# Seven products in three more places, and one step more ahead of the first scores, in a two-layer hybrid encoder

## The chip, the core and the metric

The kernel runs on one core of one Trainium2 chip. The metric is the device time of one execution in microseconds. Three runs of the kernel before took 2244.38, 2242.65 and 2243.16 us, so the median is 2243.16.

## What is computed

A trunk of two layers over 256 positions of width 2048, all in fp32: RMS-normalisation, a token mixer and a residual add, then RMS-normalisation, a gated MLP with a convolution of width 3 over positions and a residual add. Layer 0 mixes by grouped-query attention (mixer A: 16 query heads, 4 key and value heads of 128, RMS-normalised and rotated queries and keys), layer 1 by three groups of 8 heads with dilated windows (mixer B). At the end stands one more RMS-normalisation. Cut to the skeleton:

```python
def reference(x, ...):
    h = x
    for i in range(2):
        hn = rms_norm(h, mix_norm[i])
        h = h + (mixer_a(hn, ...) if i == 0 else mixer_b(hn, ...))
        h = h + conv_ffn(rms_norm(h, ffn_norm[i]), ...)
    return rms_norm(h, final_norm)

def mixer_b(h, w_qkv, w_o, rel_bias):
    qkv = (h @ w_qkv).reshape(b, s, 3, 3, 8, 128)       # group, q/k/v, head
    ...
    return y @ w_o

def conv_ffn(h, w_up, conv_w, conv_b, w_down):           # 2048 -> 2 x 5632 -> 2048
    u = conv(h @ w_up) + conv_b
    gate, val = jnp.split(u, 2, axis=-1)
    return (silu(gate) * val) @ w_down
```

## The kernel before

**Matmuls.** An fp32 matmul is made of three in the fp32r type: both operands are split in a high and a low part, and hi·hi, hi·lo and lo·hi are summed in a PSUM bank. Weights come in tiles `raw` of 128x1024 by DMAs that SyncE issues (six buffers, `NRAW`); ACT copies the high part `wh` (L128) and DVE subtracts it for the low part `wl` (L129), in `split_raw`. The two instructions get a priority (`AHEAD`) that moves them ahead in the order that the framework's scheduler writes for each engine. Three pairs `wh`, `wl` circulate, four in the down-projections. Activations lie transposed in SBUF, split in `xh`, `xl` or `ah`, `al`, and are the stationary operand; the 256 positions make two blocks of 128, `m` = 0 and 1, each with a PSUM bank of 128x512 of its own.

**Plain projection.** `feed` (L139) does 512 rows of a weight (a k-group) by 512 columns (a column block): 2 tiles, 4 rows of 128, 2 position blocks and 3 matmuls, 24 matmuls of 128x512 in two halves. `project` (L180) is a loop of feeds over the k-groups of one column block. After each half feed `step` (L90) lets the oldest of the waiting generators go on to its next `yield`: that is how the vector work of an earlier part is put between the matmuls of a later one.

**Seven products.** `project_pair` (L215) does two column blocks at once from a list of units. A unit `("c", k, i)` is one weight tile with 12 plain matmuls. Units `("P", k, p)` are the seven products of Winograd's form of Strassen's scheme for the k-group `k`, whose two position blocks and two halves of rows, and whose two halves of rows and two column blocks, make 2x2 matrices: 6 matmuls each, 42 in place of 48 for two blocks. The operands of four of the products are sums of weight tiles, which DVE makes in place (L245). The sums of activations, `forms`, are made ahead. P2, P3 and P4 add to the accumulators C11, C12 and C21 of the plain units, while P1, P5, P6 and P7 have PSUM banks of their own (M1, M5, M6, M7). `ORDER` is the order of the products, 1, 2, 5, 3, 7, 6, 4.

**Down-projection** (in `ffn`, L476). Its 11 k-groups are done in two halves, 0 to 5 and 6 to 10, each over four column blocks `n` of the residual `h`. `weave` (L670) orders the units of a pair of blocks, with the k-groups `SKG` in seven products. `combine` (L683) is a generator on DVE that adds M1, M6, M5 and M7 to `h` in four steps (L687 to L698), and `done` (L619) adds an accumulator to `h` (L624). In the last half of layer 1 `done` also squares the sum on ACT (L626) and multiplies by the final gain on GpSimd, `h` times `fin` (L627); for the last block `finish` (L641) makes the norm and the output's DMAs. In this half blocks 0 and 1 are a pair, with two k-groups of five in seven products, and blocks 2 and 3 are two plain projections.

**Mixer A** (L777). `attend` (L889) is the generator of four heads: it normalises the queries, waits three steps, transposes them (the low part `qTl` comes from DVE, L300), and then makes the scores of head 0 (`mm3`, L316 to L318), and further heads a step each.

**Mixer B** (L985). Its width of 3072 is done in two halves `hf`, so each group `g` has a key block and a query block of 512 columns per half. Groups 1 and 2 get both by `seven` (L1137): k-groups 0 to 2 in plain units, three of them ahead, k-group 3 in seven products, whose sums DVE puts together in four tiles `ms` (L1144 to L1147, L1150, L1151, L1160, L1161). Group 0 has two plain projections. The three value blocks follow.

Of the kernel before, what the change touches and what calls it, by code (L numbers as in the profile page):

```python
# [7 lines left out]
F32 = mybir.dt.float32  # L8
# [5 lines left out]
P = 128  # L14
# [14 lines left out]
LEAD = 4  # L29
# [4 lines left out]
def tile_encoder(ctx: ExitStack, tc: tile.TileContext, x, xT, w_a, w_ao, q_gain, k_gain, w_b, w_bo,  # L34
# [145 lines left out]
    def project(w, n, lhs, kgs, by_m=False, accs=None):  # L180
        accs = accs or new_acc()
        for i, kg in enumerate(kgs):
            end = i == len(kgs) - 1
            feed(accs, lhs, kg, w[n, kg], i == 0, end, by_m and end)
        return accs
# [26 lines left out]
                    first_done(a0)  # L212
        return a1

    def project_pair(w, n0, n1, lhs, forms, units, late, early_done, n0_done, product_done=None):  # L215
        home = {1: "M1", 2: "C11", 3: "C12", 4: "C21", 5: "M5", 6: "M6", 7: "M7"}
        if product_done:
            acc = dict(zip(("C11", "C21", "C12", "C22"), new_acc() + new_acc()))
# [9 lines left out]
        for i, u in enumerate(units):  # L228
            for k in touched(u):
                first.setdefault(k, i)  # L230
                last[k] = i
        blocks = {}
        sums = {5: ("11", "12"), 7: ("12", "22"), 6: ("22", "11"), 4: ("21", "22")}

# [17 lines left out]
        for i, (kind, kg, p) in enumerate(units):  # L252
# [13 lines left out]
            if kind == "c":  # L266
                for j in range(2):
                    for m, k in enumerate(touched((kind, kg, p))):
                        todo.append((k, *at(lhs[4 * kg + 2 * (p % 2) + j], m), j))
            else:  # L270
                xh, xl = forms[kg][p]
# [204 lines left out]
    def ffn(l, hT, ss_in, g_next, last, side=None):  # L476
        with tc.tile_pool(name=nm("wpool"), bufs=1) as wp, tc.tile_pool(name=nm("fpool"), bufs=1) as fp:
# [101 lines left out]
            for hf, (p0, p1) in enumerate(HALVES):  # L579
# [88 lines left out]
                cs = [("c", k, i) for k in range(np_) if k not in SKG[hf] for i in range(4)]  # L668
                ps = [("P", k, p) for k in SKG[hf] for p in ORDER]
                def weave(lead):  # L670
                    c, units = list(cs), []
                    units += [c.pop(0) for _ in range(lead)]
                    lone = (ps[0], ps[7]) if lead > 1 and hf == 0 else ()
                    for u in ps:
                        units += [u] + [c.pop(0) for _ in range(min(1, len(c))) if u not in lone]
                    return units + c
# [33 lines left out]
                def pair(n0, n1, late):  # L710
                    units = weave(LEAD if late else 1)
                    late_at = next(i for i, u in enumerate(units) if u[1] == np_ - 1)
                    acc = project_pair(wd, n0, n1, slots, forms, units, late_at if late else None,
                                       lambda a: start(combine(a, n0, n1)),
                                       lambda a: first_half(a, n0, n1))
# [12 lines left out]
            assert not spare  # L728
        return hTn, ss
# [47 lines left out]
    def mixer_a():  # L777
        with tc.tile_pool(name="apool", bufs=1) as ap:
# [110 lines left out]
            def attend(g, accs):  # L889
# [95 lines left out]
    def mixer_b(hT, ss_in):  # L985
        with tc.tile_pool(name="bpool", bufs=1) as bp:
# [26 lines left out]
            for hf in range(2):  # L1013
# [123 lines left out]
                def seven(n0, n1, sums, n0_ready, n1_ready):  # L1137
# [20 lines left out]
                    a = project_pair(w_b, n0, n1, hT, {3: hT["forms"]}, units, None, lambda a: None,  # L1158
                                     n0_done, product_done)
                    nc.vector.tensor_tensor(q0, a["C12"], q0, ALU.subtract)  # L1160
                    nc.vector.tensor_tensor(q1, a["C22"], q1, ALU.subtract)  # L1161
# [14 lines left out]
            return out_proj(w_bo, slots, [0, 2, 4, 1, 3, 5], 3, 3, junk, bp, ("vl", "kTh"))  # L1176
# [89 lines left out]
```

## Time and profile before

| | us |
|---|---|
| runs | 2244.38, 2242.65, 2243.16 |
| the profiled execution | 2242.91 |
| its span, from the first instruction to the last | 2241.1 |
| TensorE (PE) busy | 2228.8 |
| VectorE (DVE) busy | 1739.7 |
| ScalarE (ACT) busy | 1520.5 |
| GpSimd (POOL) busy | 334.4 |
| granted TensorE clock, mean | 0.999 |

A row of a timeline gives the start in us, the duration in us, the engine, the line, the operation and its tiles; in square brackets stands how long the engine was idle before, and what ended that. A row of a list of waits gives the engine, what it was to write and in which line, then what it waited for: us in total, times, longest us. A row of a group of instructions gives line, engine, operation, tiles, shapes and count, then busy us, mean ns of one, and the idle time ahead of them. Matmuls are pipelined: the next one starts before the end of the one before is written down, so the step between two starts, not the duration, is what one costs.

### The profile page before, as it was taken

How to read it: one execution, taken by the hardware profiler on the slowest of the kernel's cores; microseconds unless marked ns; L12 is line 12 of the kernel's file. 1: busy time of each engine (PE TensorE's matmuls, PEld its weight loads, DVE VectorE, ACT ScalarE, POOL GpSimd, SP SyncE). 2: the span in 40 equal slices, each digit the busy share in tenths (PEclk: the TensorE clock that was granted, in tenths of full speed). 3: DMA queues.
4: the chain of work that ended last, by engine and by line, in shares of the span. 5: the costliest groups of instructions: out<-in, count | busy, mean ns of one | idle time of the engine just before them, and what ended most of it. 6: DMA issues, size and time to landing. Idle time of an engine off the chain costs nothing.

```text
span 2241.1 us, 28999 instructions
## 1 busy us (share of the span) xinstructions
PE 2228.8 (99%) x10063; PEld 1848.4 (82%) x10063; DVE 1739.7 (78%) x2374; ACT 1520.5 (68%) x2345; POOL 334.4 (15%) x490
## 2 busy tenths in 40 slices
PE   9999999999999999999999999999999999999998
PEld 7888888888888888888888888888888888888886
DVE  6777778888878788968875877566887898688895
ACT  7665677777547777767875777556777755677763
POOL 2210211210001010121331213000110100001101
PEclk9999999999999999999999999999999999999999
DMA  8544656766665655666655565566566666556653
GB/s 303 163 144 152 207 188 207 245 201 192 216 197 186 200 189 187 213 216 207 196 184 180 169 206 173 188 193 190 191 196 192 194 206 206 188 191 194 224 197 134
DMA packets 126500, 437.45 MB, mean 195 GB/s; under 512 B 17312, under 2 KB 18080, under 8 KB 126352
## 3 DMA queue, kind: packets, MB, share of 16 engines
q1 hardware_dynamic: 119744, 425.64, 58.7%
q0 software_dynamic: 6176, 9.39, 1.7%
q8 instruction: 79, 1.29, 0.2%
q14 instruction: 69, 0.57, 0.1%
q10 hardware_dynamic: 432, 0.56, 0.1%
HBM read 429.20 MB, written 6.29 MB: 194 GB/s over the span
## 4 chain that ended last, share of the span: by engine, by line
PE 97%; DVE 1%; issue 1%; DMA 1%; ACT 0%; POOL 0%; SPq 0%; POOLq 0%; DVEq 0%
PE acc L154 24%; PE acc L155 24%; PE acc L153 24%; PE acc L279 7%; PE acc L281 7%; PE acc L284 7%; PE ps L314 1%; PE ps L318 1%; PE ps L317 1%; PE ps L316 0%; DVE wl L129 0%; PE ps L928 0%; DMA xt<-in_xT_dram 0%; PE ps L281 0%; PE ps L279 0%
## 5 line engine op out<-in xcount | busy, mean ns | idle before, releaser
L129 DVE TENSOR_TENSOR wl<-raw,wh 128x1024 fp32r<-128x1024 f32 x840 | 1033.4, 1237 | 362.8 <-ACT wh L128 360.6
L128 ACT ACTIVATE wh<-raw 128x1024 fp32r<-128x1024 f32 x840 | 885.5, 1057 | 510.8 <-PE acc L155 298.6
L153 PE MATMUL acc<-wh,xh 128*128 128x512 f32 x1920 | 748.8, 390 | 0.0
L154 PE MATMUL acc<-wl,xh 128*128 128x512 f32 x1920 | 747.7, 389 | 0.8 <-DVE wl L165 0.7
L155 PE MATMUL acc<-wh,xh 128*128 128x512 f32 x1920 | 748.0, 390 | 0.0
L154 PEld LDWEIGHTS acc<-wl,xh 128*128 128x128 f32 x1920 | 360.6, 188 | 75.3 <-DVE wl L165 1.5
L155 PEld LDWEIGHTS acc<-wh,xh 128*128 128x128 f32 x1920 | 360.4, 188 | 74.7
L153 PEld LDWEIGHTS acc<-wh,xh 128*128 128x128 f32 x1920 | 360.8, 188 | 73.4
L354 POOL COPY u<-t 32x256 f32<-32x256 f32 x176 | 110.7, 629 | 1002.8 <-DVE t L515 994.7
L279 PE MATMUL acc<-wh,ah 128*128 128x512 f32 x520 | 202.3, 389 | 0.0
L281 PE MATMUL acc<-wh,al 128*128 128x512 f32 x520 | 202.3, 389 | 0.0
L153 PE MATMUL acc<-wh,ah 128*128 128x512 f32 x480 | 187.2, 390 | 0.4 <-DVE cu L689 0.4
L154 PE MATMUL acc<-wl,ah 128*128 128x512 f32 x480 | 186.9, 389 | 0.0
L155 PE MATMUL acc<-wh,al 128*128 128x512 f32 x480 | 186.8, 390 | 0.0
L356 ACT ACTIVATE u<-t 32x256 f32<-32x256 f32 x352 | 147.7, 420 | 14.0 <-DVE t L515 6.2
L284 PE MATMUL acc<-wl,ah 128*128 128x512 f32 x520 | 145.8, 389 | 0.0
L284 PEld LDWEIGHTS acc<-wl,ah 128*128 128x128 f32 x520 | 97.6, 188 | 20.3
L281 PEld LDWEIGHTS acc<-wh,al 128*128 128x128 f32 x520 | 97.6, 188 | 20.2
L279 PEld LDWEIGHTS acc<-wh,ah 128*128 128x128 f32 x520 | 97.6, 188 | 20.2
L153 PEld LDWEIGHTS acc<-wh,ah 128*128 128x128 f32 x480 | 90.2, 188 | 19.3 <-DVE cu L689 1.0
L155 PEld LDWEIGHTS acc<-wh,al 128*128 128x128 f32 x480 | 90.1, 188 | 18.7
L154 PEld LDWEIGHTS acc<-wl,ah 128*128 128x128 f32 x480 | 90.2, 188 | 18.2
(231 smaller groups left out, 2193.3 us busy)
## 6 DMA issues: line engine op xcount, KB each, us to landing
raw<-in_w_up_dram SPq DMA_DIRECT2D x352, 512.0 KB, 4.4
raw<-in_w_down_dram SPq DMA_DIRECT2D x176, 512.0 KB, 4.7
raw<-in_w_b_dram SPq DMA_DIRECT2D x144, 512.0 KB, 4.5
raw<-in_w_bo_dram SPq DMA_DIRECT2D x48, 512.0 KB, 4.4
raw<-in_w_a_dram SPq DMA_DIRECT2D x40, 512.0 KB, 4.6
raw<-in_w_ao_dram SPq DMA_DIRECT2D x32, 512.0 KB, 3.8
raw<-in_w_a_dram SPq DMA_DIRECT2D x16, 256.0 KB, 6.3
h<-in_x_dram SPq DMA_DIRECT2D x4, 512.0 KB, 8.1
```

The source lines that it names most:

```text
L128: nc.scalar.activation(wh, r, AF.Copy)
L129: nc.vector.tensor_tensor(wl, r, wh.bitcast(F32), ALU.subtract)
L153: nc.tensor.matmul(accs[m], xh, wh[:, j, :], start=st, stop=False)
L154: nc.tensor.matmul(accs[m], xh, wl[:, j, :], start=False, stop=False)
L155: nc.tensor.matmul(accs[m], xl, wh[:, j, :], start=False, stop=sp)
L279: nc.tensor.matmul(acc[k], xh, wh[:, j, :], start=k in fresh, stop=False)
L281: nc.tensor.matmul(acc[k], xl, wh[:, j, :], start=False, stop=False)
L284: nc.tensor.matmul(acc[k], xh, wl[:, j, :], start=False, stop=last[k] == i and j == 1)
L314: nc.tensor.matmul(o, lh[ls], rh[rs], start=start, stop=stop)
L317: nc.tensor.matmul(o, lh[ls], rl[rs], start=False, stop=False)
L354: nc.gpsimd.tensor_copy(dst, src)
L356: nc.scalar.activation(dst, src, AF.Copy)
```

## The change

1. In mixer B group 0 goes by `seven` too. In the first of these calls only (half 0, `n0 == 2`) five plain units stand ahead in place of three, and P5 and P6 have no plain unit behind them. `forms` is handed over as a function, since the sums of activations aren't made yet at the time of the call.
2. In the last half of layer 1 blocks 2 and 3 are a `pair` as well, with `tail=True`: only k-group 0 in seven products, the plain units in an order of their own, and the last k-group of block 3 as a plain feed in the order of position blocks (`by_m`), as the whole last feed was before.
3. In mixer A the generator of the first four heads has one more `yield` between the transposes and the first scores.

```diff
-    def project_pair(w, n0, n1, lhs, forms, units, late, early_done, n0_done, product_done=None):
+    def project_pair(w, n0, n1, lhs, forms, units, late, early_done, n0_done, product_done=None, tail=False):
...
+        if tail:
+            last["C12"] = last["C22"] = None
...
-                def weave(lead):
-                    c, units = list(cs), []
+                def weave(lead, tail):
+                    ks = SKG[hf][:1] if tail else SKG[hf]
+                    c = [("c", k, i) for k in range(np_) if k not in ks for i in range(4)]
+                    ps = [("P", k, p) for k in ks for p in ORDER]
+                    if tail:
+                        c0, c1 = ([u for u in c if u[2] // 2 == n] for n in range(2))
+                        c = c0[:-1] + c1[:3] + c0[-1:] + c1[3:-2]
+                    units = []
...
-                    done((acc["C12"], acc["C22"]), n1)
+                    accs = acc["C12"], acc["C22"]
+                    if tail:
+                        feed(accs, slots, np_ - 1, wd[n1, np_ - 1], False, True, True)
+                    done(accs, n1)
...
-                if hf == 0:
-                    pair(2, 3, False)
+                if hf == 0 or last:
+                    pair(2, 3, False, hf == 1)
...
-                    done(project(wd, 3, slots, seq, last), 3)
+                    done(project(wd, 3, slots, seq), 3)
...
                 for _ in heads_T(qT, ro):
                     pass
+                if g == 0:
+                    yield
...
-                    units = [cs.pop(0) for _ in range(3)]
-                    for p, c in zip(ORDER, (1, 1, 1, 1, 1, 1, 3)):
+                    first = n0 == 2
+                    units = [cs.pop(0) for _ in range(5 if first else 3)]
+                    for p, c in zip(ORDER, (1, 1, 0, 1, 1, 0, 3) if first else (1, 1, 1, 1, 1, 1, 3)):
...
-                    if g == 0:
-                        start(k_gen(g, project(w_b, n0, hT, kgs)))
-                        start(s_gen(g, project(w_b, n1, hT, kgs), bts))
-                    else:
-                        sums = [[bp.tile([P, 512], F32, tag=t, name=nm("ms"), bufs=2) for _ in range(2)]
-                                for t in ("pTh", "pTl")]
-                        seven(n0, n1, sums, lambda a: start(k_gen(g, a)), lambda a: start(s_gen(g, a, bts)))
+                    sums = [[bp.tile([P, 512], F32, tag=t, name=nm("ms"), bufs=2) for _ in range(2)]
+                            for t in ("pTh", "pTl")]
+                    seven(n0, n1, sums, lambda a: start(k_gen(g, a)), lambda a: start(s_gen(g, a, bts)))
```

The program has 18 matmuls of 128x512 less on PE, 16 instructions more on ACT (nine of them splits) and 45 more on DVE (nine splits, twelve sums of weight tiles, the rest adds that combine products). The number of DMAs and of GpSimd's instructions is the same. Lines in the rows of after are 2 to 11 higher than in those of before.

PE's order in mixer A, before, from the end of a half feed into accumulators 778 and 779 (the next block of queries) to the first scores `ps` = keys `kT` times queries `qT`:

```order
L153 MATMUL acc_779<-wh_850,xh_214 128x512
L154 MATMUL acc_779<-wl_851,xh_214 128x512
L155 MATMUL acc_779<-wh_850,xh_214 128x512
L316 MATMUL ps_866<-kTh_138,qTh_776 128x256
L317 MATMUL ps_866<-kTl_139,qTh_776 128x256
L318 MATMUL ps_866<-kTh_138,qTl_777 128x256
```

And after, from the same matmul:

```order
L155 MATMUL acc_779<-wh_850,xh_214 128x512
L153 MATMUL acc_778<-wh_870,xh_261 128x512
L154 MATMUL acc_778<-wl_871,xh_261 128x512
L155 MATMUL acc_778<-wh_870,xh_261 128x512
L153 MATMUL acc_779<-wh_870,xh_261 128x512
L154 MATMUL acc_779<-wl_871,xh_261 128x512
L155 MATMUL acc_779<-wh_870,xh_261 128x512
L153 MATMUL acc_778<-wh_870,xh_264 128x512
L154 MATMUL acc_778<-wl_871,xh_264 128x512
L155 MATMUL acc_778<-wh_870,xh_264 128x512
```

A half feed of 12 matmuls, the first ten of which these are, now stands ahead of the first scores.

PE's order at the start of column blocks 2 and 3 in the last half, before; `acc_18984` is the accumulator that P4 of blocks 0 and 1 adds to, `acc_19437` and `acc_19438` those of block 2:

```order
L284 MATMUL acc_18984<-wl_19402,ah_17803 128x512 x2
L153 MATMUL acc_19437<-wh_19443,ah_17047 128x512
L154 MATMUL acc_19437<-wl_19444,ah_17047 128x512
L155 MATMUL acc_19437<-wh_19443,al_17048 128x512
L153 MATMUL acc_19437<-wh_19443,ah_17047 128x512
L154 MATMUL acc_19437<-wl_19444,ah_17047 128x512
L153 MATMUL acc_19438<-wh_19443,ah_17061 128x512
```

After, some 20 matmuls behind P4: `acc_19499` is C11 and `acc_19500` C21 of blocks 2 and 3, `acc_19496` M5; `wh_19553` is P2's weight tile, `wh_19584` that of P5:

```order
L283 MATMUL acc_19499<-wh_19553,al_17110 128x512
L286 MATMUL acc_19499<-wl_19554,ah_17109 128x512 x2
L281 MATMUL acc_19496<-wh_19584,ah_17111 128x512
L283 MATMUL acc_19496<-wh_19584,al_17112 128x512
L281 MATMUL acc_19496<-wh_19584,ah_17111 128x512
L283 MATMUL acc_19496<-wh_19584,al_17112 128x512
L281 MATMUL acc_19500<-wh_19505,ah_17453 128x512
L283 MATMUL acc_19500<-wh_19505,al_17454 128x512
L281 MATMUL acc_19500<-wh_19505,ah_17455 128x512
```

The first two units' matmuls for C21 have moved behind P1, P2 and the high part of P5, which is the 25th matmul after P4; they begin at `acc_19500<-wh_19505`, 12 in all.

DVE's order at the same place, before; `cu` is the tile of `combine`, `wl_19402` belongs to P4, and L624 adds an accumulator to `h`:

```order
L129 TENSOR_TENSOR wl_19402<-raw_19341,wh_19401 128x1024
L129 TENSOR_TENSOR wl_19444<-raw_19439,wh_19443 128x1024
L129 TENSOR_TENSOR wl_19460<-raw_19440,wh_19459 128x1024
L689 TENSOR_TENSOR cu_19411<-acc_18981,cu_19411 128x512
L129 TENSOR_TENSOR wl_19480<-raw_19475,wh_19479 128x1024
L690 TENSOR_TENSOR cu_19411<-acc_18980,cu_19411 128x512
L129 TENSOR_TENSOR wl_19496<-raw_19476,wh_19495 128x1024
L692 TENSOR_TENSOR cu_19411<-acc_18982,cu_19411 128x512
```

After; `wl_19460` belongs to P4, L247 makes the sum of weight tiles for P5, and L626 adds `acc_19042`, whose bank C21 of blocks 2 and 3 gets:

```order
L129 TENSOR_TENSOR wl_19460<-raw_19399,wh_19459 128x1024
L129 TENSOR_TENSOR wl_19506<-raw_19503,wh_19505 128x1024
L129 TENSOR_TENSOR wl_19524<-raw_19521,wh_19523 128x1024
L129 TENSOR_TENSOR wl_19536<-raw_19533,wh_19535 128x1024
L695 TENSOR_TENSOR cu_19469<-acc_19039,cu_19469 128x512
L129 TENSOR_TENSOR wl_19554<-raw_19551,wh_19553 128x1024
L696 TENSOR_TENSOR cu_19469<-acc_19038,cu_19469 128x512
L247 TENSOR_TENSOR raw_19521<-raw_19521,raw_19565 128x1024
L698 TENSOR_TENSOR cu_19469<-acc_19040,cu_19469 128x512
L699 TENSOR_TENSOR h<-h,cu_19469 128x512
L701 TENSOR_TENSOR h<-h,cu_19469 128x512
L703 TENSOR_TENSOR cu_19469<-acc_19040,cu_19469 128x512
```

The M6 add (L689 before, L695 now) has one more split ahead of it, and P5's sum of weight tiles has come in behind the M5 add (L696). The next row is the residual add of `acc_19042` (L626); an `h` minus `cu`, two more such adds and P5's low part follow.

More of the change, by code (lines that the diff above doesn't have):

```diff
@@ L270, in project_pair @@
             else:
-                xh, xl = forms[kg][p]
+                xh, xl = forms(kg)[p]
                 for j in range(2):
@@ L667, in ffn @@
                         fin.append(f)
-                cs = [("c", k, i) for k in range(np_) if k not in SKG[hf] for i in range(4)]
-                ps = [("P", k, p) for k in SKG[hf] for p in ORDER]
-                def weave(lead):
-                    c, units = list(cs), []
+                def weave(lead, tail):
[6 more added lines that the diff above has]
+                    units = []
                     units += [c.pop(0) for _ in range(lead)]
@@ L708, in first_half, with pair @@
                     done((a["C11"], a["C21"]), n0)
-                def pair(n0, n1, late):
-                    units = weave(LEAD if late else 1)
+                def pair(n0, n1, late, tail=False):
+                    units = weave(LEAD if late else 1, tail)
                     late_at = next(i for i, u in enumerate(units) if u[1] == np_ - 1)
-                    acc = project_pair(wd, n0, n1, slots, forms, units, late_at if late else None,
+                    acc = project_pair(wd, n0, n1, slots, forms.get, units, late_at if late else None,
                                        lambda a: start(combine(a, n0, n1)),
-                                       lambda a: first_half(a, n0, n1))
-                    done((acc["C12"], acc["C22"]), n1)
+                                       lambda a: first_half(a, n0, n1), tail=tail)
+                    accs = acc["C12"], acc["C22"]
+                    if tail:
+                        feed(accs, slots, np_ - 1, wd[n1, np_ - 1], False, True, True)
+                    done(accs, n1)
                     finished(n0, n1)
@@ L1154, in seven @@
                     cs = [("c", k, i) for i2 in range(2) for k in kgs[:3] for i in (2 * i2, 2 * i2 + 1)]
-                    units = [cs.pop(0) for _ in range(3)]
-                    for p, c in zip(ORDER, (1, 1, 1, 1, 1, 1, 3)):
+                    first = n0 == 2
+                    units = [cs.pop(0) for _ in range(5 if first else 3)]
+                    for p, c in zip(ORDER, (1, 1, 0, 1, 1, 0, 3) if first else (1, 1, 1, 1, 1, 1, 3)):
                         units += [("P", 3, p)] + [cs.pop(0) for _ in range(c)]
-                    a = project_pair(w_b, n0, n1, hT, {3: hT["forms"]}, units, None, lambda a: None,
+                    a = project_pair(w_b, n0, n1, hT, lambda kg: hT["forms"], units, None, lambda a: None,
                                      n0_done, product_done)
```

## The prediction

> **What bounds the kernel now.** I read the page first (busy times and the chain of work that ended last), then the list of TensorE's waits, then the timeline at the places that the change touches.
>
> ```profile
> PE 2228.8 (99%) x10063; PEld 1848.4 (82%) x10063; DVE 1739.7 (78%) x2374; ACT 1520.5 (68%) x2345; POOL 334.4 (15%) x490
> PE 97%; DVE 1%; issue 1%; DMA 1%; ACT 0%; POOL 0%; SPq 0%; POOLq 0%; DVEq 0%
> ```
>
> TensorE (PE) is busy for 2228.8 of 2241.1 us, and 97% of the chain that ended last is PE's. So a matmul less is time less, unless a wait comes in its place. The whole list of PE's waits is short:
>
> ```profile
> PE ps L456 <- DVE warm L453: 1.5, 1, 1.5
> PE acc L154 <- DVE wl L165: 0.7, 1, 0.7
> PE ps L318 <- DVE qTl L300: 0.6, 1, 0.6
> PE acc L153 <- DVE cu L689: 0.4, 1, 0.4
> ```
>
> The first two are at the start of the program, which is not changed. The third lies in mixer A and the fourth at the start of the last two column blocks: both at places of the change. No line names mixer B, whose groups 1 and 2 already run in seven products.
>
> **The change part by part.** The price of one 128x512 matmul is read as the step from one start to the next, since the durations overlap. PE's timeline in mixer A, at the third wait and at the next group of six score matmuls:
>
> ```profile
> 83.83 0.39 PE L153 MATMUL acc<-wh,xh 128*128 128x512 f32 x1
> 84.06 0.39 PE L154 MATMUL acc<-wl,xh 128*128 128x512 f32 x1
> ...
> 85.19 0.28 PE L316 MATMUL ps<-kTh,qTh 128*128 128x256 f32 x1
> 85.30 0.28 PE L317 MATMUL ps<-kTl,qTh 128*128 128x256 f32 x1
> 86.19 0.39 PE L318 MATMUL ps<-kTh,qTl 128*128 128x256 f32 x1 [0.61 <-DVE qTl L300]
> ...
> 86.77 0.40 PE L153 MATMUL acc<-wh,xh 128*128 128x512 f32 x1
> ...
> 89.52 0.28 PE L316 MATMUL ps<-kTh,qTh 128*128 128x256 f32 x1
> ...
> 90.23 0.40 PE L153 MATMUL acc<-wh,xh 128*128 128x512 f32 x1
> ```
>
> From 83.83 to 85.19 six matmuls start: 1.36 / 6 = 0.227 us each.
>
> **1, matmuls.** A k-group of two column blocks is 48 matmuls plain and 42 in seven products. The change does this for one k-group in each half of mixer B (12 matmuls less) and one in the tail (6 less): 18 x 0.227 = **-4.08 us** (-2.72 in mixer B, -1.36 in the tail).
>
> **2, mixer A.** The six scores at 85.19 take until 86.77, 1.58 us; the next six take 90.23 - 89.52 = 0.71. The wait thus costs 0.87 us, more than the 0.61 that the view names. With the extra step, 12 matmuls of the projection (2.72 us) stand between the transposes and the first scores. The scores' third matmul then comes at about 85.30 + 2.72 = 88.0, and what it waited for was there just before 86.19: it waits no more. All later steps of the heads move back by one half feed and keep their distance from each other, and DVE's order there moves along, so I price the rest at nothing: **-0.87 us**; as bounds 0 (the wait comes back at another step of the same size) and -0.87.
>
> **3, mixer B.** Its first stages, one in each half, are at 980 to 1025 and 1187 to 1232 us; the first line of three below is such a stage, the second the stage behind it, which is in seven products already; the third is the other half's. The columns are window, its length, then busy us and instructions of PE, weight loads, DVE, ACT, POOL.
>
> ```profile
> 980.00:1025.00 45.00, 45.00 (x204) 37.26 (x203) 28.72 (x35) 30.56 (x48) 11.00 (x17) 1.00 0.71 223
> 1025.00:1068.00 43.00, 43.00 (x202) 35.99 (x201) 37.72 (x41) 32.88 (x54) 11.57 (x18) 1.00 0.63 211
> 1187.00:1232.00 45.00, 45.00 (x208) 37.20 (x207) 26.24 (x27) 26.78 (x39) 6.58 (x10) 1.00 0.60 187
> ```
>
> Groups of DVE and POOL in the first window, then of DVE in the second, then of POOL in the third:
>
> ```profile
> L129 DVE TENSOR_TENSOR wl<-raw,wh 128x1024 fp32r<-128x1024 f32 x17 | 20.8, 1225 | 14.6 <-ACT wh L128 14.4
> L354 POOL COPY stg<-tT 32x256 f32<-32x256 f32 x11 | 7.2, 659 | 34.0 <-DVE tT L344 33.6
> ...
> L129 DVE TENSOR_TENSOR wl<-raw,wh 128x1024 fp32r<-128x1024 f32 x18 | 21.9, 1234 | 1.7 <-ACT wh L128 1.6
> L245 DVE TENSOR_TENSOR raw<-raw,raw 128x1024 f32<-128x1024 f32 x4 | 5.1, 1265 | 0.4 <-DMA raw<-in_w_b_dram 0.4
> L1144 DVE TENSOR_TENSOR ms<-ps,ms 128x512 f32<-128x512 f32 x1 | 0.7, 683 | 0.0
> ...
> L354 POOL COPY stg<-tT 32x256 f32<-32x256 f32 x10 | 6.8, 678 | 55.1 <-DVE tT L344 54.8
> ```
>
> Seven products add to a stage: three splits (19 weight tiles in place of 16), 3 x 1.23 = 3.7; four operand sums of 128x1024, 4 x 1.27 = 5.1; eight adds of 128x512 that combine the products, 8 x 0.68 = 5.4. That is +14.2 us of DVE, while the stage shrinks to 45.00 - 1.36 = 43.64. DVE comes to 28.72 + 14.2 = 42.9 in the first half, and to 26.24 + 14.2 = 40.4 in the second. The work fits, by 0.7 and 3.2 us: what covers it is the time in which DVE now waits for ACT (14.4 us in the first row). ACT gets three splits and three copies of products more, at most 6 x 1.07 = 6.4 us by the ACT row quoted for the tail, and comes to 37.0 of 43.64. The stage behind, with 37.72 of 43.00 and no wait of PE's in the list, shows that such a stage can run free. I take **0** for both halves; the bounds are 0 (nothing shortens a matmul) and +1.2, DVE one split late into the next stage. If DVE's room is gone, see the slower rival.
>
> One rule of the skill speaks against these adds. The Trainium skill, "SBUF — State Buffer", section "SBUF: two separate sides", says that VectorE and GpSimd share a port pair as an exclusive lock: an instruction of VectorE with two SBUF inputs and one of GpSimd that reads SBUF shut each other out for the whole instruction. By it the first stage's adds could stand behind 7.2 us of POOL's copies; the row of L129 in the same window, 1225 ns with eleven copies beside it, shows no such cost, and the second window, fuller, 1234 ns. I go by the rows.
>
> **4, the tail.** Here the plain projection is replaced by seven products right behind the last product (P4) of the pair of blocks 0 and 1, and DVE is busy there with that pair's combination. PE, DVE, POOL and ACT in the timeline of before:
>
> ```profile
> 2176.96 0.39 PE L153 MATMUL acc<-wh,ah 128*128 128x512 f32 x1
> ...
> 2177.87 0.39 PE L154 MATMUL acc<-wl,ah 128*128 128x512 f32 x1
> 2178.63 0.50 PE L153 MATMUL acc<-wh,ah 128*128 128x512 f32 x1 [0.38 <-DVE cu L689]
> 2178.97 0.39 PE L154 MATMUL acc<-wl,ah 128*128 128x512 f32 x1
> ...
> 2174.49 3.48 DVE L129 TENSOR_TENSOR wl<-raw,wh 128x1024 fp32r<-128x1024 f32 x3
> 2177.90 0.68 DVE L689 TENSOR_TENSOR cu<-acc,cu 128x512 f32<-128x512 f32 x1
> 2178.50 1.70 DVE L129 TENSOR_TENSOR wl<-raw,wh 128x1024 fp32r<-128x1024 f32 x1
> 2180.12 0.68 DVE L690 TENSOR_TENSOR cu<-acc,cu 128x512 f32<-128x512 f32 x1
> ...
> 2186.65 8.29 DVE L129 TENSOR_TENSOR wl<-raw,wh 128x1024 fp32r<-128x1024 f32 x5
> ...
> 2176.66 2.46 POOL L627 TENSOR_TENSOR h<-h,fin 128x512 f32<-128x512 f32 x1 [46.91 <-DMA raw<-in_w_down_dram]
> ...
> 2170.68 1.07 ACT L128 ACTIVATE wh<-raw 128x1024 fp32r<-128x1024 f32 x1 [1.48 <-DVE raw L245]
> ```
>
> Before, PE loses (2178.63 - 2177.87 - 0.227) + (2178.97 - 2178.63 - 0.227) = 0.65 us waiting for a bank. The sixth matmul of the block goes to the bank that M6 filled, which DVE's L689 frees. In the new order that wait is gone, since the first 24 matmuls (two units of column block 2, of its first accumulator only, P1 and P2) need no bank that is late. PE reaches the end of these at 2176.96 + 24 x 0.227 = 2182.40.
>
> What is late next stands in DVE's new order, quoted above with the change. From 2174.49, where both orders are still alike: the split of P4 and three more, 4 x 1.14 (the three in the row take 3.41 until the next start) to 2179.05; the M6 add 0.60 (2177.90 to 2178.50) to 2179.65; a split to 2180.79; the M5 add to 2181.39; the operand sum of P5 to 2182.53. Before, the split at 2178.50 took 1.70 in place of 1.14 with POOL's h times fin beside it; I add these 0.56, which gives 2183.1. ACT's wh for P5, 1.07, ends at 2184.1 to 2184.2, and PE, there at 2182.40, has waited 1.7 us. After P5's four matmuls (0.91) PE is at 2185.0 and comes to the 12 postponed matmuls of the second accumulator, whose bank is read by the residual add of the block before; on DVE that add stands behind the sum and four adds: 2183.1 + 5 x 0.60 = 2186.1, a wait of 1.1. Then 12 + 8 matmuls to 2190.6; DVE's three last adds to 2187.9 and two splits. In the row of 2186.65 five splits took 8.29, 1.66 each, beside POOL, so they end at 2191.2: 0.6 more. In sum 1.7 + 1.1 + 0.6 = 3.4 us of waits in place of 0.65, **+2.75 us**. The lower bound is -0.65 (no wait at all) if the sum is early; without any delay by POOL it is 1.1 + 1.1 + 0 = 2.2, +1.55. The upper bound is +4.0: one split of 1.2 more late, since the sixth weight tile may land after DVE's turn. The window from there to the last matmul, columns as above:
>
> ```profile
> 2176.00:2232.00 56.00, 55.62 (x245) 45.55 (x244) 37.11 (x39) 22.98 (x31) 11.11 (x7) 1.00 0.44 150
> ```
>
> DVE was busy for 37.11 of 56 us, so I see nothing that is late after these 15 us; from the last matmul on the program keeps its code.
>
> **The sum.** -4.08 - 0.87 + 0 + 2.75 = -2.2 us. The profiled execution took 2242.91 us, 0.25 less than the median of 2243.16; on the median the forecast is 2240.96, about **2241.0**, a gain of 0.1%. A measurement of this kernel tells about 0.2%, 4.5 us, from no change: 2238.7 and 2247.6 are the borders.
>
> **The rivals.**
> *The waits of the tail do not come.* An order is not a time: DVE may be early. Then the sum is -4.08 - 0.87 - 0.65 = -5.6, that is 2237.6. It is faster by over 0.2% as soon as the tail's waits stay under 1.1 us (-4.95 + (1.1 - 0.65) = -4.5). For it: in the list of waits DVE and ACT let PE stand only once after the first 100 us of the program, and here too by 0.4 us only. Against it: the sum for P5 stands behind four splits and two adds, an order that no speed of PE changes. Chance 0.25.
> *Slower: DVE becomes the bound in mixer B.* The stage of the first half has 0.7 us of room, the second's 3.2. If adds and copies there shut each other out, POOL's copies (7.2 and 6.8 us) come on top: 42.9 + 7.2 - 43.64 = 6.5 us late, and 40.4 + 6.8 - 43.64 = 3.6. With both it is 2241.0 + 10.1 = 2251.1; the decision (slower by over 0.2%) falls where three quarters of the copies' time (6.6 + 3.9 = 10.5 of 14.0) are added. The lock of the Trainium skill's page "SBUF — State Buffer", above, is this mechanism. Against it stand the mean of 1234 ns in a stage with 37.72 us of DVE, and the list of waits. Chance 0.12.
> *The step in mixer A only moves its wait.* Then -0.87 is lost: 2241.8. It lies within 0.2% like the forecast; chance 0.1.
>
> **How the numbers follow.** My forecast has 0.53 and the third rival 0.1, together 0.63 for a time within 0.2%. The first rival has 0.25: faster. The second has 0.12: slower. The forecast's own range comes from the bounds: -4.08 - 0.87 + 1.55 = -3.4 to -4.08 + 0 + 1.2 + 4.0 = +1.1, so 2239.8 to 2244.3. To hold 8 in 10 it must reach into the faster rival, to 2237.6, and a little into the slower one, to 2246.0.
>
> **What would show it.** Right: 18 matmuls of 128x512 fewer, at the same 0.227 us; no wait for qTl in mixer A; no new wait in 980 to 1070 and 1185 to 1275; in the tail two or three waits of PE, for ACT's wh of P5 (whose operand is DVE's sum) and for DVE's residual add, of 2.2 to 3.4 us together. Wrong: a longer wait for wl in mixer B, with splits of more than 1.3 us; a tail without waits, or with waits that come later than its first 15 us; a wait for scores or transposes in mixer A.

## The result, and the profile after

The changed kernel takes 2248.80 us (median of 10 runs, 2247.5 to 2251.1), the kernel before 2243.16 (10 runs, 2242.5 to 2244.38): 1.0026 times as long, 95% interval 1.0018 to 1.0035. It is slower by 5.6 us where 2.2 us of gain were forecast. The profiled execution took 2249.72 us, 6.8 more than that of before. Two executions of e4 (5695 and 10047 us) and one of e12 (2433 us) took far longer than the rest, and the medians below leave them out. Busy time of PE, and the chain of work that ended last, from the page of after:

```profile
PE 2228.1 (99%) x10045; PEld 1845.6 (82%) x10045; DVE 1777.1 (79%) x2419; ACT 1531.9 (68%) x2361; POOL 344.6 (15%) x490
PE 93%; DVE 3%; POOL 1%; DMA 1%; issue 1%; ACT 0%; SPq 0%; POOLq 0%; DVEq 0%; ACTq 0%
```

PE has its 18 matmuls less, and still its share of the chain has fallen from 97 to 93%, in favour of DVE and POOL. The list of PE's waits, in which four lines stood before:

```profile
PE ps L318 <- DVE al L302: 3.5, 3, 1.2
PE acc L281 <- ACT wh L128: 2.1, 2, 1.1
PE ps L939 <- DVE pr L931: 1.5, 3, 0.5
PE ps L458 <- DVE warm L455: 1.5, 1, 1.5
PE acc L154 <- DVE wl L165: 1.0, 1, 1.0
PE acc L281 <- DVE h L626: 0.6, 1, 0.6
PE acc L153 <- DVE cu L695: 0.5, 1, 0.5
PE ps L320 <- DVE qTl L302: 0.2, 1, 0.2
```

The first and third lie in mixer A, three times each, 5.0 us. The wait for qTl is gone there; the 0.2 us of the last line came at 1042.56 us, in the first half of mixer B. To see what a place costs, I took every step from one matmul's start to the next of over 0.28 us in both traces and summed what lies above 0.227:

| place | before, us | after, us | difference |
|---|---|---|---|
| start, to 20 us | 4.05 | 4.23 | +0.2 |
| mixer A, 84 to 210 us | 2.79 | 7.84 | +5.05 |
| layer 0's last down-projection, 920 us | 0.00 | 1.03 | +1.0 |
| mixer B's groups, 980 to 1310 us | 1.93 | 3.33 | +1.4 |
| the tail, from 2170 us | 0.65 | 3.85 | +3.2 |

With -4.08 for the matmuls that is +6.8, as measured. The wait at 920 us is no part of the change: its place has the same code, and in the traces of the runs below it was between 0 and 1.04 us, without regard to what was edited.

### The profile page after: what moved, and what is told of

Its sections match the earlier page's. It is cut to its first block, busy times and chain, and to the rows that moved or that the text cites. A ratio compares the mean times of both kernels' runs of the same rounds, so it can differ in the third digit from the quotient of the medians.

```text
span 2247.9 us, 29043 instructions
## 1 busy us (share of the span) xinstructions
PE 2228.1 (99%) x10045; PEld 1845.6 (82%) x10045; DVE 1777.1 (79%) x2419; ACT 1531.9 (68%) x2361; POOL 344.6 (15%) x490
## 4 chain that ended last, share of the span: by engine, by line
PE 93%; DVE 3%; POOL 1%; DMA 1%; issue 1%; ACT 0%; SPq 0%; POOLq 0%; DVEq 0%; ACTq 0%
PE acc L155 22%; PE acc L154 22%; PE acc L153 22%; PE acc L281 8%; PE acc L283 8%; PE acc L286 8%; POOL stg L356 1%; DVE wl L129 1%; PE ps L316 1%; DMA xt<-in_xT_dram 1%; DMA raw<-in_w_down_dram 0%; PE ps L318 0%; PE ps L320 0%; PE ps L319 0%; PE ps L283 0%
## 5 line engine op out<-in xcount | busy, mean ns | idle before, releaser
L154 PE MATMUL acc<-wl,xh 128*128 128x512 f32 x1792 | 697.9, 389 | 1.0 <-DVE wl L165 1.0
L153 PE MATMUL acc<-wh,xh 128*128 128x512 f32 x1792 | 698.5, 390 | 0.0
L155 PE MATMUL acc<-wh,xh 128*128 128x512 f32 x1792 | 698.0, 390 | 0.0
L154 PEld LDWEIGHTS acc<-wl,xh 128*128 128x128 f32 x1792 | 336.6, 188 | 70.7 <-DVE wl L165 1.8
L155 PEld LDWEIGHTS acc<-wh,xh 128*128 128x128 f32 x1792 | 336.4, 188 | 69.7
L153 PEld LDWEIGHTS acc<-wh,xh 128*128 128x128 f32 x1792 | 336.6, 188 | 68.7 <-ACT wh L164 0.3
L281 PEld LDWEIGHTS acc<-wh,ah 128*128 128x128 f32 x590 | 111.2, 189 | 25.7 <-ACT wh L128 1.5
L283 PEld LDWEIGHTS acc<-wh,al 128*128 128x128 f32 x590 | 111.2, 188 | 23.0
L286 PEld LDWEIGHTS acc<-wl,ah 128*128 128x128 f32 x590 | 111.1, 188 | 23.1
L281 PE MATMUL acc<-wh,xh 128*128 128x512 f32 x312 | 122.3, 392 | 1.0 <-ACT wh L128 1.0
L283 PE MATMUL acc<-wh,xh 128*128 128x512 f32 x312 | 121.5, 390 | 0.0
L247 DVE TENSOR_TENSOR raw<-raw,raw 128x1024 f32<-128x1024 f32 x76 | 93.6, 1231 | 12.6 <-DMA raw<-in_w_down_dram 12.1
```

Source lines behind the costliest of these rows:

```text
L153: nc.tensor.matmul(accs[m], xh, wh[:, j, :], start=st, stop=False)
L154: nc.tensor.matmul(accs[m], xh, wl[:, j, :], start=False, stop=False)
L155: nc.tensor.matmul(accs[m], xl, wh[:, j, :], start=False, stop=sp)
L247: nc.vector.tensor_tensor(dst, dst, src, ALU.add)
L281: nc.tensor.matmul(acc[k], xh, wh[:, j, :], start=k in fresh, stop=False)
L283: nc.tensor.matmul(acc[k], xl, wh[:, j, :], start=False, stop=False)
```

## The experiments

Theory S: the losses of the table belong each to its own part of the change, and the step in mixer A is the largest. Its rivals: D (DVE is too full, and the waits in mixer A are a by-product), and P (the prediction). Medians and ratios to the kernel before, measured beside it on the same chip:

| run | us | before, us | ratio, 95% interval |
|---|---|---|---|
| e1 no step | 2244.22 | 2243.13 | 1.0005, 0.9997 to 1.0014 |
| e2 step only | 2248.22 | 2243.13 | 1.0023, 1.0014 to 1.0033 |
| e3 mixer B only | 2242.34 | 2243.13 | 0.9996, 0.9988 to 1.0005 |
| e4 tail only | 2245.08 | 2243.13 | 1.0011, 1.0001 to 1.0020 |
| e5 step moved | 2242.73 | 2243.34 | 0.9997, 0.9988 to 1.0006 |
| e6 all shifted | 2244.55 | 2243.34 | 1.0006, 0.9997 to 1.0015 |
| e7 first half only | 2242.11 | 2243.34 | 0.9995, 0.9986 to 1.0004 |
| e8 tail, banks exchanged | 2244.15 | 2243.34 | 1.0004, 0.9995 to 1.0013 |
| e9 tail, products put off | 2243.99 | 2243.08 | 1.0004, 0.9995 to 1.0012 |
| e10 copies moved to DVE | 2241.29 | 2243.08 | 0.9993, 0.9985 to 1.0002 |
| e11 e5 and e7 | 2241.35 | 2243.08 | 0.9993, 0.9984 to 1.0001 |
| e12 e5, e7 and e9 | 2242.63 | 2243.08 | 0.9997, 0.9989 to 1.0006 |
| e13 e8 without products | 2241.66 | 2243.14 | 0.9995, 0.9986 to 1.0003 |
| e14 e4 without products | 2243.82 | 2243.14 | 1.0003, 0.9995 to 1.0012 |
| e15 e5 and e10 | 2240.30 | 2243.14 | 0.9987, 0.9978 to 0.9996 |
| e16 e15, e8, products later | 2238.45 | 2243.32 | 0.9980, 0.9971 to 0.9989 |

Many intervals hold 1; there the sign rests on the medians with the waits of the traces, not on the ratio.

### One part at a time

e1 is the changed kernel less this; e2 is the kernel before with it; e3 and e4 are the kernel before with the first and the second part of the change's diff:

```diff
-                if g == 0:
-                    yield
```

> The changed kernel without the extra step in mixer A (parts 1 and 2 alone). Theory S, the step itself costs: the trace of after loses 2.9 to 7.9 us of matmul pitch in mixer A, so taking the step away gives back 5.0 us: 2248.8 - 5.0 = 2243.8 us, and the wait for qTl (0.6) is back while those for pr and al are gone. Rival D, DVE is too full in mixer B and the tail, and mixer A's waits are a by-product that varies: 2247 to 2249 us. Rival P, the prediction, by which the step gains 0.87: 2249.7 us.

> The kernel before with the extra step in mixer A alone. Theory S: 2243.2 + 5.0 = 2248.2 us, with three waits for pr (L931 of after) and three for al, two in each of the last three blocks of queries. Rival D: 2243 us. Rival P: 2242.3 us.

> The kernel before with the seven products of mixer B's group 0 alone. Theory S, by the trace of after: -2.72 for 12 matmuls, +0.26 and +1.23 us of waits in the stages behind: 2243.2 - 1.2 = 2242.0 us. Rival D, DVE as the bound there: 2246 us or more. Rival P, no wait at all: 2240.4 us.

> The kernel before with the seven products of the last two column blocks alone. Theory S, by the trace of after, where the tail lost 3.85 us to waits in place of 0.65: -1.36 + 3.2 = +1.8, so 2245.0 us. Rival P, the prediction's waits of 3.4: 2244.6 us, which this run can hardly tell apart; if the tail's waits were a result of the other parts: 2241.2 to 2241.8 us.

Measured: 2244.2, 2248.2, 2242.3 and 2245.1 us, each within half a microsecond of theory S. The rivals miss e1 by 3 to 6 us and e2 by 5 to 6. So the step alone costs 5.1 us, the tail 2.0, and mixer B gains 0.8; that adds up to 6.3, where the whole change lost 5.6, a gap smaller than the intervals. In the trace of e2 mixer A loses 7.84 us, as in after.

### Why a step costs 5 us in mixer A

The timeline of after at the last steps of the first four heads; L868, L875 and L876 turn the next block's queries and square them, L931 is the last head's softmax, L302 the low parts for PE. PE's two waits first, then DVE:

```profile
107.58 0.63 PE L939 MATMUL ps<-ident,pr 128*128 128x128 f32 x4 [0.49 <-DVE pr L931]
112.81 0.36 PE L318 MATMUL ps<-pTh,vh 128*128 128x256 f32 x1 [1.18 <-DVE al L302]
...
101.96 1.33 DVE L868 TENSOR_TENSOR ro<-stg,ct_q 128x1024 f32<-128x1024 f32 x1
...
104.77 1.21 DVE L875 TENSOR_TENSOR ro<-ro,t 128x1024 f32<-128x1024 f32 x1
105.90 0.15 DVE L929 RECIPROCAL l<-l 128x2 f32<-128x2 f32 x1
105.98 1.19 DVE L876 TENSOR_REDUCE ssq<-sq 128x8 f32<-128x1024 f32 x1
107.09 0.60 DVE L931 TENSOR_SCALAR pr<-pr,l 128x256 f32<-128x256 f32 x2
...
110.43 0.17 DVE L900 TENSOR_SCALAR rqk<-rqk 128x8 f32<-128x8 f32 x1 [1.53 <-POOL rqk L452]
110.51 1.23 DVE L129 TENSOR_TENSOR wl<-raw,wh 128x1024 fp32r<-128x1024 f32 x1
111.65 0.68 DVE L302 TENSOR_TENSOR pTl<-ps,pTh 128x512 fp32r<-128x512 f32 x1
```

The same two pieces of work in before, the softmax (L920 there) and the first of the rotation (L859):

```profile
102.64 0.61 DVE L920 TENSOR_SCALAR pr<-pr,l 128x256 f32<-128x256 f32 x2
104.43 1.40 DVE L859 TENSOR_TENSOR ro<-stg,ct_q 128x1024 f32<-128x1024 f32 x1 [1.17 <-ACT stg L747]
```

The generator of a block's heads is one step longer, but the next block's query work starts when its projection ends, which no step moves. So the rotation, which came behind the last softmax, now stands ahead of it on DVE, and the last low part stands behind L900, where DVE itself waits 1.53 us for GpSimd. Both waits come again in each block (L318 and L939 three times). Theory C is this collision; rival R holds the later heads themselves responsible.

```diff
# e5: one of the three steps ahead of the transposes goes behind them
                 yield
                 yield
-                yield
+                if g > 0:
+                    yield
                 for _ in heads_T(qT, ro):
                     pass
+                if g == 0:
+                    yield
# e6: the change's step, and the query work of blocks 1 to 3 a step later
             def attend(g, accs):
+                if g > 0:
+                    yield
                 ro, rq = qk_post(accs, "q")
```

> The kernel before, with the first heads' transposes one step earlier and the step gained put between them and the first scores: the same gap of 12 matmuls ahead of the scores as in the change, but no step of the heads behind them moves. Theory C, the change's waits in mixer A come from a collision on DVE: the heads are one step later, so their last softmax stands behind the next block's rotation of queries. Then these waits don't come here and 0.9 us is gained: 2242.3 us. If the transposes are now too early for the queries, PE waits for them instead, up to half a feed of 2.7 us: 2245 us. Rival R, the gap itself is what disturbs the heads: 2248 us.

> The kernel before with the change's step in mixer A and one more yield ahead of the query work of blocks 1 to 3, so that the rotation of the next block's queries is late by one step too and everything keeps its distance. Theory C: the waits for pr and al go and the gain for qTl stays, 2242.3 us. Rival R, heads that are one step later meet a fuller part of the feeds, whatever the next block does: 2248 us.

e5 took 2242.7 us: no head is later, there is no wait in mixer A, and the gain of 0.6 us for qTl is there. So the gap of 12 matmuls does no harm, against rival R. e6 took 2244.6, between the two: the waits for al went, those for pr stayed. Its DVE and PE:

```profile
104.68 1.21 DVE L859 TENSOR_TENSOR ro<-stg,ct_q 128x1024 f32<-128x1024 f32 x1
105.82 0.15 DVE L922 RECIPROCAL l<-l 128x2 f32<-128x2 f32 x1
105.89 1.19 DVE L867 TENSOR_REDUCE ssq<-sq 128x8 f32<-128x1024 f32 x1
107.01 0.60 DVE L924 TENSOR_SCALAR pr<-pr,l 128x256 f32<-128x256 f32 x2
...
107.49 0.63 PE L932 MATMUL ps<-ident,pr 128*128 128x128 f32 x4 [0.49 <-DVE pr L924]
```

The scheduler put two of the rotation's instructions ahead of the last softmax all the same, and PE waits for that softmax; the rest of the rotation came later and no longer delays PE. This agrees with theory C, though the edit did only a part of what it was for; why the scheduler chose this order stays open.

### Mixer B: the second half waits for GpSimd

In after PE waits once in the second half. Rows of GpSimd (copies that turn the queries of group 0), ACT and PE:

```profile
1227.68 5.29 POOL L356 COPY stg<-tT 32x256 f32<-32x256 f32 x8 [52.16 <-DVE tT L346]
1234.61 8.11 POOL L356 COPY stg<-tT 32x256 f32<-32x256 f32 x8 [1.64 <-DVE tT L346]
...
1242.75 1.06 ACT L301 ACTIVATE qTh<-stg 128x1024 fp32r<-128x1024 f32 x1 [1.55 <-POOL stg L356]
1243.72 1.04 ACT L128 ACTIVATE wh<-raw 128x1024 fp32r<-128x1024 f32 x1
...
1244.81 0.50 PE L281 MATMUL acc<-wh,xh 128*128 128x512 f32 x1 [0.95 <-ACT wh L128]
```

And GpSimd's copies of this half in before, first the keys', then the queries':

```profile
1207.79 4.46 POOL L354 COPY stg<-tT 32x256 f32<-32x256 f32 x8 [37.51 <-DVE tT L344]
1229.55 6.17 POOL L354 COPY stg<-tT 32x256 f32<-32x256 f32 x8 [17.30 <-DVE tT L344]
```

There the two sets stand 22 us apart; in after the keys' copies begin at 1227.68, since seven products finish both blocks close together, and the queries' follow at once, at 1.01 us each in place of 0.77. ACT waits for them, and the split behind is late for PE. Theory G says that this chain is the cause.

```diff
# e7: seven products in group 0 of the first half only
+                    if g == 0 and hf == 1:
+                        start(k_gen(g, project(w_b, n0, hT, kgs)))
+                        start(s_gen(g, project(w_b, n1, hT, kgs), bts))
+                        continue
# e10: both halves; four of the eight block copies on DVE
-                    yield from heads_T_dve(qT, qs, bp, "vl", "papa")
+                    yield from heads_T_dve(qT, qs, bp, "vl", "pava" if (g, hf) == (0, 1) else "papa")
```

> The kernel before with seven products in mixer B's group 0 for the first half alone. By the trace of the run with both halves the first one costs 0.2 and the second 1.2 us of new waits for 1.36 us of matmuls each: 2243.1 - 1.36 + 0.2 = 2242.0 us, and no wait of PE between 1187 and 1280 us but those of before. Rival D, both halves fill DVE alike and what is late in one is late in the other: half of the gain of both, 2242.7 us.

> Mixer B's change alone (both halves), and the turning of the queries of group 0 in the second half done with four block copies on GpSimd in place of eight, the other four on DVE. Theory G, PE's wait of 1.1 us there comes through ACT, whose split stands behind qTh, and that behind eight copies of GpSimd of 1.01 us each: the wait goes, 2242.3 - 1.1 = 2241.2 us. Rival D, DVE is too full there: the copies it gets make its splits late, 2242.3 us or more.

e7 2242.1 us, e10 2241.3: both as theory G has it. In e10 GpSimd and ACT read:

```profile
1228.37 3.50 POOL L356 COPY stg<-tT 32x256 f32<-32x256 f32 x4 [1.64 <-DVE tT L346]
...
1235.10 1.06 ACT L301 ACTIVATE qTh<-stg 128x1024 fp32r<-128x1024 f32 x1
```

GpSimd is done 3 us ahead of ACT, which no longer waits; DVE had room for the copies it was given.

### The tail: two waits, and a slower clock

PE, DVE and POOL in after:

```profile
2188.80 0.50 PE L281 MATMUL acc<-wh,ah 128*128 128x512 f32 x1 [1.11 <-ACT wh L128]
...
2190.63 0.80 PE L281 MATMUL acc<-wh,ah 128*128 128x512 f32 x1 [0.63 <-DVE h L626]
2191.22 0.63 PE L283 MATMUL acc<-wh,al 128*128 128x512 f32 x1
2191.65 0.63 PE L281 MATMUL acc<-wh,ah 128*128 128x512 f32 x1
...
2184.12 1.72 DVE L129 TENSOR_TENSOR wl<-raw,wh 128x1024 fp32r<-128x1024 f32 x1
...
2181.15 3.61 POOL L629 TENSOR_TENSOR h<-h,fin 128x512 f32<-128x512 f32 x1 [46.28 <-ACT junk L628]
```

Windows of 1 us of after, where the third number from the end is the granted clock:

```profile
2189.00:2190.00 1.00, 0.99 (x4) 0.47 (x3) 1.00 (x3) 0.95 (x1) 0.00 (x0) 1.00 0.00 0
2190.00:2191.00 1.00, 0.37 (x1) 0.37 (x2) 1.00 (x2) 0.39 (x1) 0.00 (x0) 0.78 0.00 0
2191.00:2192.00 1.00, 1.00 (x3) 0.79 (x3) 1.00 (x3) 0.81 (x3) 0.59 (x1) 0.50 0.00 0
...
2193.00:2194.00 1.00, 1.00 (x4) 0.81 (x3) 0.94 (x2) 1.00 (x2) 0.00 (x0) 0.51 0.00 0
2194.00:2195.00 1.00, 1.00 (x5) 0.82 (x5) 1.00 (x1) 0.63 (x3) 0.51 (x1) 1.00 0.00 0
```

The two waits that were forecast, for P5's weight tile and for the residual add, are there: 1.27 and 0.80 us lost. In the place of the third the granted clock falls to 0.50 for 3.4 us, and the matmuls start 0.43 us apart (2191.22, 2191.65). That is 1.7 us of the 3.85. GpSimd's product beside DVE's splits takes 3.61 us, and the split beside it 1.72.

e1 has the same tail and shows what comes without the slower clock. Its PE rows with a wait, and its window of 20 us:

```profile
2184.20 0.50 PE L281 MATMUL acc<-wh,ah 128*128 128x512 f32 x1 [1.10 <-ACT wh L128]
2186.03 0.50 PE L281 MATMUL acc<-wh,ah 128*128 128x512 f32 x1 [0.64 <-DVE h L626]
2191.49 0.73 PE L286 MATMUL acc<-wl,ah 128*128 128x512 f32 x2 [0.62 <-DVE wl L129]
```

```profile
2180.00:2200.00 20.00, 17.63 (x75) 13.49 (x74) 20.00 (x21) 10.36 (x15) 4.82 (x4) 1.00 0.34 116
```

The first two waits are those of after, 1.27 and 0.80 us lost, but the clock stays at 1.00, and the third wait, for a split, comes as forecast. This tail loses 3.27 us, so with the slower clock in place of the third wait the profiled execution of after lost only 0.6 us more.

```diff
# e8: banks of the tail's pair
+            at_banks = (2 - b, 5, 3 - b, 7, 4, 6, b, b + 1) if tail else (4, 5, 6, 7, 2 - b, 3 - b, b, b + 1)
# e9: e8, and the products h times fin for n = 0 and 1 put into the code for n = 2
# e13: e8, e14: e4, both without these four products
+                                if n == 2:
                                     nc.gpsimd.tensor_tensor(hs, hs, fin[n], ALU.mult)
```

> The seven products of the last two column blocks alone, with C11 and C21 in the banks that M1 and M6 of the pair before had, and M1 and M6 in the banks of its C11 and C21. Now no matmul of C21 is put off behind P5, so 12 more stand ahead of P5's weight tile. Theory B, PE waits because of the bank and the order that it makes: the waits of 4.1 us fall to 1 or 2, 2242.7 to 2243.5 us. Rival D, DVE has more to do in these 15 us than they hold, whatever the banks are: the waits move on to a later split and stay at 3 to 4 us, 2244.5 to 2245.3 us.

> The tail with the exchanged banks, and GpSimd's products h times fin for the column blocks 0 and 1 put off until block 2 is done, so that none runs beside the combination of blocks 0 and 1. Theory L, DVE is late in the tail because these products of GpSimd and DVE's splits shut each other out (three splits took 6.37 us, 2.1 each, beside 5.75 us of them): the splits fall to 1.15, the waits of 2.3 us nearly go, 2244.2 - 2.2 = 2242.0 us. Rival D, DVE has too many instructions there, whatever GpSimd does: 2244 us. If the products put off now disturb the last block: 2244 us or more, with waits after 2210 us.

e8 took 2244.2 us, between its two answers: the wait for P5 and that for the bank went, but 2.3 us came at two splits behind them. e9 took 2244.0, but says nothing on theory L: the scheduler took the products up to where they had been (at 2186.41 in its trace). e12, which carries the same edit, misses for the same reason:

> Seven products in group 0 of the first half of mixer B, and the first heads' transposes one step earlier; the tail is that of before. If the parts add up: 2243.2 - 1.2 - 0.6 = 2241.4 us.

> The same with the tail of seven products, exchanged banks and GpSimd's products put off. By theory L: 2241.4 - 1.36 - 0.65 + 0.3 = 2239.7 us; by rival D: 2242.4 us.

e11 took 2241.4 us, so the parts for the mixers add up; e12 took 2242.6. To settle it, the products were taken away:

> The tail with the exchanged banks (2244.2 us), and the four products of GpSimd with the final gain for column blocks 0 and 1 left out, so this part of the output lacks the gain. Theory L: no split beside them takes over 1.3 us, the waits of 2.3 us fall under 0.5: 2242.0 to 2242.4 us. Rival D: splits become shorter and waits stay, since the combination's adds stand ahead of them all the same: 2243.7 us or more.

> The change's own tail alone (2245.3 us), with the same four products left out. Theory L: the operand sum of P5 and the residual add come 0.6 us sooner, the waits of 2.1 us fall to 1.5, and the granted clock may stay at 1.00 in place of 0.50 for 3 us: 2243.1 to 2244.7 us. Rival D: the waits for P5 and for the residual add stay and the clock falls as before: 2245.3 us.

2241.7 and 2243.8 us: theory L in both. The three splits and the three products beside them in e8, then the three splits in e13:

```profile
2187.01 6.37 DVE L129 TENSOR_TENSOR wl<-raw,wh 128x1024 fp32r<-128x1024 f32 x3
...
2186.55 5.75 POOL L630 TENSOR_TENSOR h<-h,fin 128x512 f32<-128x512 f32 x3 [7.08 <-ACT junk L629]
```

```profile
2189.15 3.48 DVE L129 TENSOR_TENSOR wl<-raw,wh 128x1024 fp32r<-128x1024 f32 x3
```

3.48 us in place of 6.37, and e13 has no wait of PE in the tail. In e14 the two waits stay, 0.8 us each, the third is gone, and the clock does not fall; as it doesn't in e1 either, the clock says nothing on theory L. The tail of e14 loses 1.79 us in place of the 3.27 of e1: the products cost 1.5, and the order and the bank keep the rest. PE's rows with a wait there:

```profile
2184.56 0.50 PE L281 MATMUL acc<-wh,ah 128*128 128x512 f32 x1 [0.60 <-ACT wh L128]
2186.39 0.50 PE L281 MATMUL acc<-wh,ah 128*128 128x512 f32 x1 [0.64 <-DVE h L626]
```

### A version that beats both

e15 joins e5 and e10. e16 adds the tail with e8's banks and holds the products back by a value that is ready after block 2 only:

```diff
# e16, in done, for n == 2, behind the two lines that make part
+                            for m in range(2):
+                                for q in range(2):
+                                    hq = h[:, m, q * 512:(q + 1) * 512]
+                                    nc.vector.scalar_tensor_tensor(hq[:, :1], part[:, m:m + 1], 0.0, hq[:, :1],
+                                                                   ALU.mult, ALU.add)
+                                    nc.gpsimd.tensor_tensor(hq, hq, fin[q], ALU.mult)
```

> Both halves of mixer B in seven products with four block copies on DVE in the second (2241.3 us), and the first heads' transposes one step earlier (0.6 less): 2240.7 us if the parts add up. The tail is that of before.

> The version of e15 for the mixers, the tail of seven products with the exchanged banks, and the four products of GpSimd held back until block 2 is done: DVE first adds zero times the mean square to one column of their operand. Nothing is left out. Theory L: the tail gains its 6 matmuls and the wait for the bank, 1.36 to 2.0 us less than 2240.3 of e15: 2238.3 to 2239.0 us. If the products then lock DVE beside the last block, or are late for the end: 2240 us or more, with waits after 2215 us or a longer way from the last matmul to the end than 9.3 us.

2240.3 and 2238.5 us, 0.13% and 0.20% faster than before. The products of e16 run where DVE has little to do, and there is no wait in the tail:

```profile
2218.08 6.01 POOL L644 TENSOR_TENSOR h<-h,fin 128x512 f32<-128x512 f32 x4
```

## Why the prediction was wrong, by its steps

1. **Matmuls.** Right: 18 fewer, at 0.227 us. e16 has the same 18 fewer without new waits in mixer A and the tail, and e13 the 6 of the tail: this gain can be had.
2. **Mixer A.** This is the step that failed: "All later steps of the heads move back by one half feed and keep their distance from each other, and DVE's order there moves along, so I price the rest at nothing". The wait for qTl went from mixer A as forecast, but the steps' distance to the next block's query work did not stay. +5.05 us stood where -0.87 was forecast: 5.9 of the 9.0 us by which the profiled execution misses the sum. The rival that the step only moves its wait had the right kind of effect and priced it at 0; it counted one wait where three blocks have two each. The order of DVE after, in which L868 stands ahead of L931, was there to be read before.
3. **Mixer B.** Taken at 0 with +1.2 as the upper bound; +1.4 was measured, 0.2 of it in the first half (a new wait for qTl). The rival had the two engines that shut each other out, but not the way to PE: DVE was not the bound. GpSimd's copies for keys and queries came close together and slow, ACT waited for them in order, and a split of ACT was late.
4. **The tail.** The mechanism was right and the size near: +3.2 in place of +2.75, and +2.6 in e1, whose clock did not fall. The two waits cost 2.07 us in place of 2.8. The third, 0.6 in the sum, came as 0.62 in e1; in the profiled execution of after a slower clock, which no term held, took its place with 1.7. The row of 2178.50 had shown how DVE and GpSimd delay each other, and the sum priced it there (0.56). The tail's gain of 2.0 us (1.36 of matmuls, 0.65 of the old wait) went to two causes, each nearly enough alone: e14, with the change's banks and order but without the products, loses 1.79 us, and e8, with the products and other banks, 2.31. With neither (e13, e16) the tail has no wait.

The rest, +1.0 at 920 us and +0.2 at the start, varies from one execution to the next.

## What to carry to other kernels

When a step is put into a chain of generators, list what does not move with it, and look in the new order of each engine for pairs that have changed places; the distance within the chain says nothing on that. Before adding work to VectorE, look for GpSimd instructions beside it: two engines that are each half free can make each other late. Read single durations there, since a mean over a stage hides the few that waited. Code put later in a program is not later where a scheduler orders by readiness; a data dependence is.

## What was not expected of the hardware

**The clock.** In after two waits, 1.27 and 0.80 us, in 3.3 us with four matmuls between them, came just before the granted clock halved for 3.4 us; in e4 they were 1.73 and 0.81. But e1 has the waits of after, with the same four matmuls between them, and keeps its clock, as e14 does after 0.76 and 0.80 us. So the size of the waits doesn't decide it alone; what does stays open. The Trainium skill, "TensorE: Matmul & The Clock Gate", section "Part 1: The HAM clock gate", names an idle window of about 3.4 us for this; in after PE was idle for some 60% of such a time (2.07 of 3.4, an estimate by the page's figure), with work in between.

**The lock.** The rule of the Trainium skill, "SBUF — State Buffer", section "SBUF: two separate sides", which the prediction weighed and left, holds in these runs: splits of 2.1 us beside GpSimd's products and of 1.16 without (6.37 / 3, 3.48 / 3), products of 3.61 us beside DVE's splits and of 1.27 beside adds that read a PSUM bank (2191.41 us in after). In e8 the two take turns:

```profile
2187.81 2.26 POOL L630 TENSOR_TENSOR h<-h,fin 128x512 f32<-128x512 f32 x1
2188.85 2.31 DVE L129 TENSOR_TENSOR wl<-raw,wh 128x1024 fp32r<-128x1024 f32 x1
2190.03 2.27 POOL L630 TENSOR_TENSOR h<-h,fin 128x512 f32<-128x512 f32 x1
```

Each begins while the one before still runs, but they end 1.1 us apart, at 2190.07, 2191.16 and 2192.30: about what one takes alone. Adds that read a PSUM bank were not hit; splits and operand sums, with both inputs in SBUF, were. The row that spoke against the rule, splits of 1225 ns beside eleven copies, held the cost on GpSimd's side: in the trace of before eight of these copies took 0.39 to 0.40 us, and three, at 1001.79, 1022.68 and 1024.54 us beside a split or an operand sum, 1.29 to 1.42.
